# The factor of a gated recurrence's RMS norm as one power on GpSimd instead of a root on ScalarE and a reciprocal with correction on VectorE

## The chip, the cores and the metric

The kernel runs on one core of a Trainium2 chip. The metric is the device time of one execution in microseconds (us), the median of several runs. A core has four computing engines that work side by side and wait for one another through semaphores: TensorE (PE in the profile, with its weight loads as PEld), VectorE (DVE), ScalarE (ACT) and GpSimd (POOL). SyncE (SP) issues DMAs here. Each engine takes its instructions in a fixed order.

## The reference

Two layers, each a half-step SwiGLU feed-forward block, a mixing block with two branches, and a second feed-forward block, over 272 tokens (16 meta tokens and 256 of the sequence) of width 1024. One branch of the mixing block is multi-head attention with 8 heads over latent vectors, the other a gated linear recurrence with 4 heads of 128 channels. The change is in the norm at the recurrence's end:

```
o = o * lax.rsqrt(jnp.mean(o * o, axis=-1, keepdims=True) + EPS) * norm_w.astype(f32)
gate = jax.nn.silu(g_in.astype(f32)).reshape(B, L, HG_HEADS, HG_VDIM)
return (o * gate).reshape(B, L, HG_WIDTH).astype(dt)
```

For each head and token, the mean over 128 channels of the squares goes through a power of -1/2, and the result scales the head's output.

## The kernel before

Everything lies transposed: channels on the 128 partitions, tokens along the free dimension, 272 columns wide (256 in the last layer for all that only the 256 output tokens need). Each weight piece arrives by DMA in fp32 (`raw`) and is split into a rounded high part by ScalarE (`wh`, L191) and a low part by VectorE (`wl`, L192); activations are split in the same way (L217, L218). A product is then three fp32r matmuls (L212 to L214), and a tile of the projections into 128 channels is 24 of these in a row.

The code is written as Python generators that are advanced in turns, and each `yield` ends a turn. In the mixing block `weave("awr", ...)` takes one turn each of the attention (a: one head's scores, and the transposes of the head before), of the gate projections (w: one tile of 24 matmuls, with its evacuation by VectorE at L734) and of the recurrence (r). This sequence of turns is the program's order; a scheduler in the framework then moves instructions within the reach of their dependences, by its own estimates of their durations, and so fixes the order of each engine. A round below is one turn of each.

In the attention turn the two score blocks of a head (L769) go to PSUM; VectorE adds the mask (L771) and takes the row maximum (L773); ScalarE takes the exponential with a sum (L774); VectorE takes the sum's reciprocal (L775) and scales a part (L776, L781), ScalarE scales the other (L779, a copy with a scale); TensorE transposes the result `pm` (L787 to L789), and ScalarE evacuates it (L791). Behind the last exponential, `gate_on` (L1047) puts 16 sigmoids over the finished gate tiles, with a load of ScalarE's table ahead.

The recurrence's end is `outputs()`. Its last steps, in the program's order:

- the squares of the four heads' outputs are summed over channels by four matmuls (L998) into one PSUM tile, 32 partitions for each head;
- L1000, VectorE: `m`, the mean plus epsilon, 128x272;
- a `yield`, then `rsqrt` (L350): root on ScalarE (L353, with a table load before it and another, L774, before the next exponential), reciprocal on VectorE (L354); a `yield`; then on VectorE one step of Newton's correction, L356, L357 and L358, which writes the factor `rg`;
- four matmuls with `rowsel` (L1006) spread each head's factor over 128 partitions, two into PSUM tiles `aux`, two into `mm`;
- VectorE multiplies these with the gated outputs and the norm's weight (L1008), and the results are split (L217, L218) for the projection that follows after the attention's end.

`rsqrt` is used by the other norms too (`Norm.rstd`, `latent_norm`), which the change leaves alone. GpSimd does little: the diagonal blocks of the recurrence (L946), copies of the rotary key (L640), and, at the end of the program, two powers of 128x1 (L462) with `ex`, a column of -0.5.

Of the kernel before, what the change touches and what calls it, by code (L numbers as in the profile page):

```python
# [10 lines left out]
F32 = mybir.dt.float32  # L11
# [3 lines left out]
ALU = mybir.AluOpType  # L15
# [3 lines left out]
P = 128  # L19
# [4 lines left out]
L = SEQ + NM  # L24
# [28 lines left out]
def trunk(ctx: ExitStack, tc: tile.TileContext, a: dict):  # L53
# [5 lines left out]
    def T(shape, dt=F32, tag=None, bufs=1):  # L59
        counter[0] += 1  # L60
        return sb.tile(shape, dt, name=f"{tag}_{counter[0]}", tag=tag, bufs=bufs)

    def PS(tag="mm"):
        counter[0] += 1
        return pp.tile([P, 512], F32, name=f"p{tag}_{counter[0]}", tag=tag, bufs=4)
# [23 lines left out]
    @contextmanager  # L89
    def hold():  # L90
        Engine.held = True
        yield
        Engine.held = False

    V, S, E, GP = Engine(nc.vector), Engine(nc.scalar), Engine(nc.tensor), nc.gpsimd
# [4 lines left out]
    def act(dt=F32):  # L100
        return T([P, L], dt, "act", 44)

    def tmp(shape=(P, L), tag="tmp", bufs=7, dt=F32):
        return T(list(shape), dt, tag, bufs)
# [98 lines left out]
    def piece():  # L203
        used[0] += 1
        while len(ready) < min(used[0] + ahead[0], len(plan)):
            ready.append(prepare(*plan[len(ready)]))
        r, ready[used[0] - 1] = ready[used[0] - 1], None
        return r
# [12 lines left out]
    ones = T([P, P], F32, "ones")  # L221
    V.memset(ones, 1.0)
    busy = T([P, 1], F32, "busy")
    S.activation(out=busy, in_=ones[:, 0:1], func=AF.Sqrt)
    ps = PS("aux")
    for _ in range(11):
# [39 lines left out]
    def col(i):  # L266
        return cols[:, i:i + 1]
# [83 lines left out]
    def rsqrt(out, m, c):  # L351
        y, z = tmp(), tmp()
        S.activation(out=y[:, c], in_=m, func=AF.Sqrt)  # L353
        V.reciprocal(out=y[:, c], in_=y[:, c])  # L354
        yield
        V.tensor_tensor(out=z[:, c], in0=y[:, c], in1=y[:, c], op=ALU.mult)  # L356
        V.scalar_tensor_tensor(out=z[:, c], in0=z[:, c], scalar=-0.5, in1=m, op0=ALU.mult, op1=ALU.mult)  # L357
        V.scalar_tensor_tensor(out=out, in0=z[:, c], scalar=1.5, in1=y[:, c], op0=ALU.add, op1=ALU.mult)  # L358
# [86 lines left out]
    def ffn_out(norm, c):  # L445
        gain = [T([P, 512], F32, "vt", 3) for _ in range(2)]
        for i in range(2):
            src = a["vecs"][FN + 4 * i:FN + 4 * i + 4].rearrange("k p -> (k p)")
            nc.scalar.dma_start(out=gain[i], in_=src.unsqueeze(0).broadcast_to([P, 512]))

        fm = T([P, 2, 4], F32, "fm")
        ex = T([P, 1], F32, "ex")
        GP.memset(ex, -0.5)
        acts = ffn_up(norm, c)

        def square(t, ps):
            S.activation(out=sqs[:, t], in_=ps, func=AF.Square, accum_out=fm[:, t, 1:2])


        def store(t, n):  # L460
            r = fm[:, t, 3:4]
            GP.tensor_tensor(out=r, in0=r, in1=ex, op=ALU.pow)  # L462
            o, (g0, g1) = ot[:, t], scaled[t]
            S.activation(out=o[:, 0:n], in_=g0[:, 0:n], func=AF.Copy, scale=r)
            if n < 512:
                V.tensor_scalar(out=o[:, n:512], in0=g0[:, n:512], scalar1=r, scalar2=None, op0=ALU.mult)
            V.tensor_scalar(out=o[:, 512:D], in0=g1, scalar1=r, scalar2=None, op0=ALU.mult)
            for q, cc in ((nc.scalar, slice(0, n)), (nc.sync, slice(n, D))):
                q.dma_start(out=a["out"][0, t * P:(t + 1) * P, cc], in_=o[:, cc])

        scaled = [[], []]
        for hf in range(2):
            pst = [PS(), PS()]

            def prods(t, k0, w):
                ts_ = slice(t * P, (t + 1) * P)
                for k in range(k0, k0 + 2):
                    (ah, al), (wh, wl) = acts[k], w[k - k0]
                    E.matmul(pst[t], ah[:, ts_], wh, start=k == 0, stop=False)  # L479
                    E.matmul(pst[t], al[:, ts_], wh, start=False, stop=False)  # L480
                    E.matmul(pst[t], ah[:, ts_], wl, start=False, stop=k == NF - 1)  # L481

            held = []
            for k0 in range(0, NF, 2):
                w = piece()
                prods(0, k0, w)
                if hf and k0 >= NF - 6:
                    held.append((k0, w))
                else:
                    prods(1, k0, w)  # L490
                for t in range(2):
                    for k in range(4 if k0 == 0 else 0):
                        E.matmul(pst[t][:, k * P:(k + 1) * P], h[4 * hf + k][:, slice(*TOK[1 + t])], ident,
                                 start=False, stop=False)
            for k0, w in held:
                prods(1, k0, w)
            sqs, os = (T([P, 2, 512], F32, n) for n in ("gq", "gk" if hf else "gf"))
            if hf == 0:
                for t in range(2):
                    square(t, pst[t])  # L500
                    V.tensor_scalar(out=fm[:, t, 0:1], in0=fm[:, t, 1:2], scalar1=1.0 / D, scalar2=EPS,
                                    op0=ALU.mult, op1=ALU.add)
                    V.tensor_tensor(out=os[:, t], in0=pst[t], in1=gain[0], op=ALU.mult)
                    scaled[t].append(os[:, t])
        ot = T([P, 2048], F32, "raw", 3).rearrange("p (t d) -> p t d", t=2)
        for t in range(2):
            scaled[t].append(os[:, t])
        with hold():
            for t in range(2):
                square(t, pst[t])  # L510
                V.tensor_tensor(out=os[:, t], in0=pst[t], in1=gain[1], op=ALU.mult)
                V.scalar_tensor_tensor(out=fm[:, t, 3:4], in0=fm[:, t, 1:2], scalar=1.0 / D, in1=fm[:, t, 0:1],
                                       op0=ALU.mult, op1=ALU.add)
                store(t, 384 if t else 512)


    def mix(l, norm, nxt):
        last = l == DEPTH - 1
        ca = slice(0, L)
        cq = slice(NM, L) if last else ca  # L520
# [454 lines left out]
        def outputs():  # L975
            og, sqs = [], []
            pss = [PS(t) for t in ("aux", "aux", "mm", "mm")]

            for g in range(G):
                ms = slice(32 * g, 32 * g + NM)  # L980
                if not last:
                    E.matmul(pss[g][:, 0:NM], gv[0][ms], amm[ms], start=True, stop=True)
                E.matmul(pss[g][:, NM:L], gv[0][ms], am[ms], start=True, stop=False)
            for g in range(G):
                gs = slice(g * P, (g + 1) * P)
                ps = pss[g]
                E.matmul(ps[:, NM:L], gv[1][:, gs], at[:, g, 1:3], start=False, stop=False)
                E.matmul(ps[:, 144:L], gv[2][:, gs], at[:, g, 0], start=False, stop=True)
                sq, o = tmp(), act()
                S.activation(out=sq[:, cq], in_=ps[:, cq], func=AF.Square)  # L990
                V.tensor_tensor(out=o[:, cq], in0=ps[:, cq], in1=gate[g][:, cq], op=ALU.mult)
                og.append(o)
                sqs.append(sq)
                if g % 2:
                    yield
            ss = PS("aux")
            for g in range(G):
                E.matmul(ss[32 * g:32 * g + 32, cq], ones[:, 0:32], sqs[g][:, cq], start=True, stop=True)  # L998
            m, rg = tmp(), act()
            V.tensor_scalar(out=m[:, cq], in0=ss[:, cq], scalar1=1.0 / P, scalar2=EPS, op0=ALU.mult, op1=ALU.add)  # L1000
            yield
            yield from rsqrt(rg[:, cq], m[:, cq], cq)
            pss = [PS(t) for t in ("aux", "aux", "mm", "mm")]
            for g in range(G):
                gs = slice(32 * g, 32 * g + 32)
                E.matmul(pss[g][:, cq], rowsel[gs], rg[gs, cq], start=True, stop=True)  # L1006
            for g in range(G):
                V.scalar_tensor_tensor(out=og[g][:, cq], in0=pss[g][:, cq], scalar=col(HGN + l), in1=og[g][:, cq],  # L1008
                                       op0=ALU.mult, op1=ALU.mult)
                oh, ol = act(F32R), act(F32R)  # L1010
                split(og[g][:, cq], oh, ol, cq)
                ob.append((oh[:, cq], ol[:, cq]))
            yield
# [186 lines left out]
```

## Time and profile before

| what | value |
|---|---|
| median of 3 runs | 1212.39 us (1212.19 to 1212.58) |
| the profiled execution's own time | 1212.17 us |
| its span in the profile | 1210.1 us |
| PE busy, DVE busy | 1196.1 us (99%), 871.0 us (72%) |
| ACT busy, POOL busy | 647.6 us (54%), 27.9 us (2%) |
| `rsqrt` of the recurrence | once a layer, around 337 to 346 us and 938 to 947 us of the span |

Busy time is the time in which an engine executes instructions. A row of the timeline gives an instruction's start, its duration, its engine and line, what it writes and reads, and in brackets the idle time of the engine just before it with what ended that. Rows of one engine overlap a little, because the next instruction starts while the last is still writing. The matmuls of L769, L998, L1006 and L812, whose operands are plain fp32, stand in the trace as two rows each.

### The profile page before, as it was taken

To read this page: it belongs to the slowest core of one execution; us is meant where nothing else is said; L and a number is where in the kernel's file an instruction comes from. 1 tells how busy PE (TensorE), PEld (TensorE's weight loads), DVE (VectorE), ACT (ScalarE), POOL (GpSimd) and SP (SyncE) were. 2 spreads that over 40 slices of the span, in tenths; PEclk is the share of its full clock that TensorE was granted. 3 is DMA by queue.
4 is the path that set the end of the run, shared out by engine and by line. 5 is a ranking of instruction groups with operands and counts; after the bars stand their busy time and mean duration, and the time that the engine had idled before them with its cause. 6 is when DMAs were issued, how large, how long until landed. Compare 5 with 4: busy or idle time off the path is not lost.

```text
span 1210.1 us, 24079 instructions
## 1 busy us (share of the span) xinstructions
PE 1196.1 (99%) x10080; PEld 1164.9 (96%) x10080; DVE 871.0 (72%) x1533; ACT 647.6 (54%) x1068; POOL 27.9 (2%) x41
## 2 busy tenths in 40 slices
PE   9999999999999999999999999999999999999997
PEld 9999999999989999999999999999989899999986
DVE  7977655898787777775568776558877787877643
ACT  5644444676684554444445444446767745554432
POOL 2000000003000000000000000000020000000000
PEclk9999999999999999999999999999999999999999
DMA  8554655554435545555554646555554355555651
GB/s 264 175 194 155 200 187 159 156 162 143 138 113 167 174 141 185 163 193 179 187 174 140 200 149 200 185 159 164 156 173 135 126 172 183 172 179 172 209 190 53
DMA packets 187052, 203.49 MB, mean 168 GB/s; under 512 B 3412, under 2 KB 174624, under 8 KB 186944
## 3 DMA queue, kind: packets, MB, share of 16 engines
q1 hardware_dynamic: 186224, 200.87, 51.8%
q8 instruction: 79, 1.29, 0.5%
q10 hardware_dynamic: 720, 1.09, 0.3%
q14 instruction: 29, 0.24, 0.1%
HBM read 200.89 MB, written 1.05 MB: 167 GB/s over the span
## 4 chain that ended last, share of the span: by engine, by line
PE 96%; DVE 2%; ACT 1%; issue 0%; POOL 0%; POOLq 0%; DVEq 0%
PE pmm L212 21%; PE pmm L214 21%; PE pmm L213 20%; PE paux L212 7%; PE paux L213 7%; PE paux L214 6%; PE pmm L481 2%; PE pmm L479 2%; PE pmm L480 2%; PE paux L84 1%; PE paux L769 1%; PE pmm L84 1%; PE paux L404 0%; PE paux L407 0%; PE pmm L404 0%
## 5 line engine op out<-in xcount | busy, mean ns | idle before, releaser
L191 ACT CAST wh<-raw 128x1024 fp32r<-128x1024 f32 (+3 forms) x390 | 391.6, 1008 | 373.0 <-PE pmm L213 252.2
L192 DVE TENSOR_TENSOR wl<-raw,wh 128x1024 fp32r<-128x1024 f32 (+3 forms) x390 | 458.5, 1179 | 184.4 <-ACT wh L191 182.8
L212 PE MATMUL pmm<-x,wh 128*128 128x272 f32 (+1 forms) x1232 | 357.7, 290 | 0.0
L214 PE MATMUL pmm<-x,wl 128*128 128x272 f32 (+1 forms) x1232 | 352.1, 286 | 0.0
L213 PE MATMUL pmm<-x,wh 128*128 128x272 f32 (+1 forms) x1232 | 352.0, 286 | 0.0
L214 PE MATMUL pmm<-act,wl 128*128 128x272 f32 (+1 forms) x836 | 239.1, 287 | 1.6 <-DVE wl L192 1.5
L212 PE MATMUL pmm<-act,wh 128*128 128x272 f32 (+1 forms) x836 | 239.8, 287 | 0.0
L213 PE MATMUL pmm<-act,wh 128*128 128x272 f32 (+1 forms) x836 | 239.2, 286 | 0.0
L212 PEld LDWEIGHTS pmm<-x,wh 128*128 128x128 f32 x1232 | 232.2, 188 | 2.2 <-ACT wh L191 0.9
L213 PEld LDWEIGHTS pmm<-x,wh 128*128 128x128 f32 x1232 | 232.5, 189 | 0.5
L214 PEld LDWEIGHTS pmm<-x,wl 128*128 128x128 f32 x1232 | 232.1, 188 | 0.0
L213 PE MATMUL paux<-x,wh 128*128 128x272 f32 (+1 forms) x640 | 183.0, 286 | 0.0
L212 PE MATMUL paux<-x,wh 128*128 128x272 f32 (+1 forms) x640 | 182.9, 286 | 0.0
L214 PE MATMUL paux<-x,wl 128*128 128x272 f32 (+1 forms) x640 | 182.6, 285 | 0.0
L214 PEld LDWEIGHTS pmm<-act,wl 128*128 128x128 f32 x836 | 157.1, 188 | 1.7 <-DVE wl L192 1.6
L212 PEld LDWEIGHTS pmm<-act,wh 128*128 128x128 f32 x836 | 157.4, 188 | 0.3 <-issue 0.2
L213 PEld LDWEIGHTS pmm<-act,wh 128*128 128x128 f32 x836 | 157.4, 188 | 0.0
L214 PEld LDWEIGHTS paux<-x,wl 128*128 128x128 f32 x640 | 120.5, 188 | 0.0
L212 PEld LDWEIGHTS paux<-x,wh 128*128 128x128 f32 x640 | 120.3, 188 | 0.0
L213 PEld LDWEIGHTS paux<-x,wh 128*128 128x128 f32 x640 | 120.3, 188 | 0.0
L217 ACT CAST act<-tmp 128x272 fp32r<-128x272 f32 (+1 forms) x88 | 36.6, 416 | 126.7 <-DVE tmp L386 126.6
L382 DVE TENSOR_TENSOR tmp<-pmm,rstd 128x272 f32<-128x272 f32 (+1 forms) x88 | 38.3, 435 | 43.3 <-PE pmm L214 42.9
(303 smaller groups left out, 1218.2 us busy)
## 6 DMA issues: line engine op xcount, KB each, us to landing
raw<-ffn_w_gu SPq DMA_DIRECT2D x86, 1024.0 KB, 5.5
raw<-w_in SPq DMA_DIRECT2D x36, 1024.0 KB, 5.3
raw<-ffn_w_down SPq DMA_DIRECT2D x34, 1024.0 KB, 5.0
raw<-ffn_w_down SPq DMA_DIRECT2D x12, 768.0 KB, 4.3
raw<-w_out SPq DMA_DIRECT2D x8, 1024.0 KB, 4.9
raw<-w_proj_attn SPq DMA_DIRECT2D x4, 1024.0 KB, 5.1
raw<-w_proj_rec SPq DMA_DIRECT2D x4, 1024.0 KB, 5.2
raw<-w_ukv SPq DMA_DIRECT2D x2, 1024.0 KB, 5.0
```

What stands on the lines that cost most here:

```text
L84: self.last = f(*args, **kw)
L191: S.copy(out=hw, in_=x)
L192: V.tensor_tensor(out=lw, in0=x, in1=hw.bitcast(F32), op=ALU.subtract)
L212: E.matmul(ps, wh, xh, start=start, stop=False)
L213: E.matmul(ps, wh, xl, start=False, stop=False)
L214: E.matmul(ps, wl, xh, start=False, stop=stop)
L217: S.copy(out=hi_tile[:, c], in_=src)
L382: V.tensor_tensor(out=gt[:, c], in0=pg[:, c], in1=r[:, c], op=ALU.mult)
L479: E.matmul(pst[t], ah[:, ts_], wh, start=k == 0, stop=False)
L480: E.matmul(pst[t], al[:, ts_], wh, start=False, stop=False)
L481: E.matmul(pst[t], ah[:, ts_], wl, start=False, stop=k == NF - 1)
L769: E.matmul(ps[:, 0:n], qs[hd][0:DQK, TOK[i + 1][0]:TOK[i + 1][1]], kT[hd][0:DQK, 0:n], start=True, stop=True)
```

## The change

The recurrence's norm no longer calls `rsqrt`. One instruction on GpSimd raises `m` to the power of -0.5, elementwise over 128x272 (128x256 in the last layer), with the exponent broadcast from a column `mhalf`. Between `m` and the `rowsel` matmuls there were two `yield`s, and now there are three. `mhalf` is filled once at the start, and the tail's two powers of 128x1 read it in place of `ex`.

```
+    mhalf = T([P, 1], F32, "mhalf")
+    GP.memset(mhalf, -0.5)
...
-        ex = T([P, 1], F32, "ex")
-        GP.memset(ex, -0.5)
+        ex = mhalf
...
             V.tensor_scalar(out=m[:, cq], in0=ss[:, cq], scalar1=1.0 / P, scalar2=EPS, op0=ALU.mult, op1=ALU.add)
             yield
-            yield from rsqrt(rg[:, cq], m[:, cq], cq)
+            GP.tensor_tensor(out=rg[:, cq], in0=m[:, cq], in1=mhalf.broadcast_to([P, L])[:, cq], op=ALU.pow)
+            yield
+            yield
             pss = [PS(t) for t in ("aux", "aux", "mm", "mm")]
```

Lines behind the edits have moved by 2 or 3: L1006 is L1009 in the changed kernel, L774 is L775, L779 is L780, L1047 is L1050. The numbers in the names are buffers and differ between the kernels.

TensorE in the first layer, before: the end of a gate tile, the `rowsel` matmuls, then the scores of the eighth head and the transposes of the seventh (`pm_4439`, `pm_4440`).

```order
L213 MATMUL pmm_4463<-x_2550,wh_4342 128x272
L214 MATMUL pmm_4463<-x_2549,wl_4343 128x272
L1006 MATMUL paux_4499<-act_4378,cst_82 128x272
L1006 MATMUL paux_4500<-act_4378,cst_82 128x272
L1006 MATMUL pmm_4501<-act_4378,cst_82 128x272
L1006 MATMUL pmm_4502<-act_4378,cst_82 128x272
L769 MATMUL paux_4529<-act_3848,act_3587 128x144
L769 MATMUL paux_4537<-act_3848,act_3587 128x272
L787 MATMUL paux_4545<-ident_77,pm_4439 128x128
```

And after: the `rowsel` matmuls (L1009) stand behind the next gate tile, with the eighth head's transposes (`pm_4495`, `pm_4496`) right behind them.

```order
L213 MATMUL pmm_4519<-x_2552,wh_4407 128x272
L214 MATMUL pmm_4519<-x_2551,wl_4408 128x272
L1009 MATMUL paux_4550<-act_4380,cst_84 128x272
L1009 MATMUL paux_4551<-act_4380,cst_84 128x272
L1009 MATMUL pmm_4552<-act_4380,cst_84 128x272
L1009 MATMUL pmm_4553<-act_4380,cst_84 128x272
L788 MATMUL paux_4578<-ident_79,pm_4495 128x128
L789 MATMUL paux_4578<-ident_79,pm_4496 128x128
L790 MATMUL paux_4578<-ident_79,pm_4496 128x128
```

So one more round (the eighth head's two scores, three transposes and 24 matmuls of a gate tile) lies ahead of `rowsel`. In the last layer the same has moved in the same way.

ScalarE in the first layer, before, from the weight split that stands ahead of the root:

```order
L191 CAST wh_4466<-raw_4464 128x1024
L353 ACT_TABLE_LOAD
L353 ACTIVATE tmp_4435<-tmp_4377 128x272
L774 ACT_TABLE_LOAD
L774 ACTIVATE pm_4380,sm_4024<-paux_4382,sm_4024 128x144
L791 COPY ptt_4402<-paux_4398 128x384
L191 CAST wh_4552<-raw_4464 128x1024
L774 ACTIVATE pm_4381,sm_4024<-paux_4390,sm_4024 128x272
```

And after, from the same weight split: the root and the two table loads are gone, and the sixth head's two exponentials follow each other with their scaling.

```order
L191 CAST wh_4465<-raw_4463 128x1024
L792 COPY ptt_4404<-paux_4400 128x384
L775 ACTIVATE pm_4382,sm_4026<-paux_4384,sm_4026 128x144
L775 ACTIVATE pm_4383,sm_4026<-paux_4392,sm_4026 128x272
L780 ACTIVATE pm_4383<-pm_4383,sm_4026 128x256
L191 CAST wh_4520<-raw_4463 128x1024
```

ScalarE after, two rounds on, at the eighth head's exponentials:

```order
L775 ACTIVATE pm_4495,sm_4026<-paux_4497,sm_4026 128x144
L775 ACTIVATE pm_4496,sm_4026<-paux_4505,sm_4026 128x272
L1050 ACT_TABLE_LOAD
L1050 ACTIVATE act_3671<-act_3671 128x272
L780 ACTIVATE pm_4496<-pm_4496,sm_4026 128x256
L191 CAST wh_4623<-raw_4585 128x1024
```

The gates' table load and first sigmoid (L1050), which stood behind that head's scaling (L779), now stand between its last exponential and its scaling (L780). On GpSimd the power is one new row in each layer, behind the copies of the rotary key and ahead of nothing in the same layer.

## The prediction

> **What bounds the kernel now.** The page's first part comes first, then the busy time by stages around the two changed places, then the list of waits.
>
> ```profile
> PE 1196.1 (99%) x10080; PEld 1164.9 (96%) x10080; DVE 871.0 (72%) x1533; ACT 647.6 (54%) x1068; POOL 27.9 (2%) x41
> 326.00:377.00 51.00, 49.23 (x397) 45.56 (x396) 37.58 (x93) 34.02 (x74) 0.00 (x0) 1.00 0.32 104
> 927.00:975.00 48.00, 45.92 (x386) 42.40 (x385) 36.07 (x92) 33.78 (x74) 0.00 (x0) 1.00 0.37 122
> PE paux L1006 <- DVE act L358: 2.9, 2, 1.6
> PE paux L787 <- DVE pm L781: 0.9, 2, 0.5
> ```
>
> TensorE is busy for 99% of the span. So work taken from VectorE and ScalarE is worth nothing by itself; only TensorE's idle time can be won. In the stretches that hold the ends of the two recurrences (second and third row: length, then busy time of PE, PEld, DVE, ACT, POOL) TensorE idles 51.00 - 49.23 = 1.77 us and 48.00 - 45.92 = 2.08 us, **3.85 us** together. The waits explain it: 2.9 us at L1006 (the `rowsel` matmuls) for L358, the last step of `rsqrt`, and 0.9 us at L787 (a transpose) for the softmax scaling on VectorE. That is the ceiling of any gain here, 0.32% of the time.
>
> The timeline of the first layer shows where these waits come from, here TensorE's anchors.
>
> ```profile
> 335.59 0.67 PE L998 MATMUL paux<-tmp,ones 128*32 128x272 f32 x8
> 336.19 0.97 PE L769 MATMUL paux<-act,act 96*128 96x144 f32 x4
> 340.32 0.87 PE L769 MATMUL paux<-act,act 96*128 96x144 f32 x4
> 345.80 0.50 PE L1006 MATMUL paux<-act,cst 32*128 32x272 f32 x2 [1.28 <-DVE act L358]
> 351.51 0.30 PE L787 MATMUL paux<-ident,pm 128*128 128x128 f32 x1 [0.49 <-DVE pm L781]
> ```
>
> And the chain on VectorE and ScalarE in between:
>
> ```profile
> 336.38 0.44 DVE L1000 TENSOR_SCALAR tmp<-paux 128x272 f32<-128x272 f32 x1 [0.23 <-PE paux L998]
> 336.64 1.28 ACT L353 ACT_TABLE_LOAD   x1
> 337.94 0.43 ACT L353 ACTIVATE tmp<-tmp 128x272 f32<-128x272 f32 x1
> 338.38 1.28 ACT L774 ACT_TABLE_LOAD   x1
> 338.49 1.84 DVE L354 RECIPROCAL tmp<-tmp 128x272 f32<-128x272 f32 x1
> 342.61 0.42 DVE L356 TENSOR_TENSOR tmp<-tmp 128x272 f32<-128x272 f32 x1
> 343.28 0.43 DVE L357 SCALAR_TENSOR_TENSOR tmp<-tmp,tmp 128x272 f32<-128x272 f32 x1
> 345.32 0.43 DVE L358 SCALAR_TENSOR_TENSOR act<-tmp,tmp 128x272 f32<-128x272 f32 x1
> ```
>
> From `m` at 336.82 to the factor at 345.75 pass 8.93 us, of which `rsqrt`'s own five steps are only 0.43 + 1.84 + 0.42 + 0.43 + 0.43 = 3.55 us. The rest is queueing: the page's chain of waits runs through VectorE almost without a hole from L1000 to L787. VectorE is the bound for those 15 us, and TensorE pays for it at two places.
>
> **What the change removes.** Per layer, VectorE loses L354 and L356 to L358, 1.84 + 0.42 + 0.43 + 0.43 = 3.12 us, and ScalarE loses two table loads and the root, from 336.64 to 339.66, 3.0 us. The sixth head's exponentials, which stood behind these table loads, come up to 3 us earlier, its `pm` with them. Both engines then reach every later step of these rounds ahead of TensorE, so I take away both waits in each layer: 3.85 us.
>
> **What it moves.** `rowsel` goes one round back. The start of the sixth head's scores at 336.19 and of the seventh's at 340.32 give a round's length on TensorE, 4.13 us. Before, `rowsel` was due at 345.80 - 1.28 = 344.52, two rounds behind 336.19 (344.45). After, it is due at 336.19 + 3 x 4.13 = 348.58. The last layer has the same pattern:
>
> ```profile
> 937.26 0.97 PE L769 MATMUL paux<-act,act 96*128 96x144 f32 x4
> 941.24 0.87 PE L769 MATMUL paux<-act,act 96*128 96x144 f32 x4
> 937.45 0.42 DVE L1000 TENSOR_SCALAR tmp<-paux 128x256 f32<-128x256 f32 x1 [0.23 <-PE paux L998]
> ```
>
> A round is 3.98 us, so `rowsel` is due at 937.26 + 3 x 3.98 = 949.20. No DMA of SP moves in order. Behind `rowsel`, VectorE's four products (L1008) and the splits come some 2.5 us later by the clock than before. They are read only by the projection after the attention's end, but the attention's copy of the probabilities (L806) is queued behind them on VectorE:
>
> ```profile
> 355.50 0.44 DVE L806 COPY act<-paux 128x272 f32<-128x272 f32 x1
> 358.40 0.74 PE L812 MATMUL paux<-act,vt 32*128 32x272 f32 x8
> ```
>
> Its reader on TensorE starts nearly 3 us behind it; TensorE reaches that reader about 1.5 us sooner now. I count nothing for it; if that cover were gone, it would cost about a microsecond a layer.
>
> **A new wait.** The order after puts the eighth head's transposes right behind `rowsel`, and on ScalarE the gates' table load and first sigmoid now stand ahead of that head's scaling (L779). The fifth head's round tells how long a softmax takes from its scores; the gates' own rows give the rest.
>
> ```profile
> 331.45 0.87 PE L769 MATMUL paux<-act,act 96*128 96x144 f32 x4
> 334.61 0.20 ACT L774 ACTIVATION_READ_ACCUMULATOR pm<-paux,sm 128x1 f32 x1
> 335.10 0.51 ACT L779 ACTIVATE pm<-pm,sm 128x256 f32<-128x256 f32 x1 [0.29 <-DVE sm L775]
> 353.01 1.28 ACT L1047 ACT_TABLE_LOAD   x1
> 354.30 0.43 ACT L1047 ACTIVATE act<-act 128x272 f32<-128x272 f32 x1
> ```
>
> From the scores to the last exponential's end are 334.81 - 331.45 = 3.36 us; with the table load, the sigmoid and the scaling, 1.28 + 0.43 + 0.51, `pm` is ready 5.58 us behind the scores. TensorE needs it a round and the `rowsel` matmuls later, 4.13 + 0.7 + 0.11 = 4.94 us. By this the wait is 0.64 us. That round had an L192 and two L991 on VectorE ahead of its maximum, which the eighth head's hasn't, so it may also be nothing. I take 0.35 us a layer, 0.7 us in all.
>
> **The power itself.** No row shows a power of 128x272. What GpSimd shows:
>
> ```profile
> 2.54 0.10 POOL L453 MEMSET ex<- 128x1 f32 x1
> 9.71 1.10 POOL L319 TENSOR_TENSOR tmp<-h 128x272 f32<-128x272 f32 x1 [7.07 <-ACT h L84]
> 10.78 0.64 POOL L319 TENSOR_TENSOR nacc<-h 128x272 f32<-128x272 f32 x1
> 1205.21 0.56 POOL L462 TENSOR_TENSOR fm<-fm,ex 128x1 f32<-128x1 f32 x1 [3.57 <-DVE fm L84]
> ```
>
> The lower end is a multiplication of the same shape, 0.64 us, or 1.10 us beside a busy VectorE. The upper end takes all of the 128x1 power beyond a bare start (0.56 - 0.10 = 0.46 us) for one column, with no overlap of columns: 272 x 0.46 = 125 us. What counts is a limit between: GpSimd is idle here, the power can start when `m` is written, and TensorE asks for it at 348.58 - 336.82 = 11.76 us (first layer) and 949.20 - 937.87 = 11.33 us (last) later. Less 0.2 us for the two handovers (my estimate from L1000's 0.23 us of idling for L998), the power is covered up to **11.5 and 11.1 us**, about 41 ns a column. That is 10 to 17 times the multiplication and a tenth of the upper end. The nearest row in operation says that most of 0.56 us can be start and latency, the nearest row in shape says about 1 us. I take it as covered, some microseconds, and keep both ends: at T us beyond the cover, the time is 1212.17 - 3.85 + 2T - 22.6 = 1185.7 + 2T.
>
> There is a rule that speaks against it. The Trainium skill's GPSIMD Engine Reference, section "Performance pitfalls for Q7 kernels", gives a chain of dependent fp32 operations as 4 cycles an element on the chain, and its section "Specifications" 1.2 GHz. An estimate from that page: 272 x 4 / 1.2 = 0.91 us for each dependent step, so that 12 steps would fill the cover, and 40 steps, 36 us, would give about 1258 us by the formula. Whether the power's loop overlaps its columns, no run here shows; by the row of 0.56 us alone both remain possible.
>
> GpSimd's work also touches VectorE's. Beside the copies of L640 a weight split took longer than in the rounds of the change:
>
> ```profile
> 296.42 6.67 POOL L640 COPY act<-act 32x272 f32<-32x272 f32 x8
> 299.35 1.42 DVE L192 TENSOR_TENSOR wl<-raw,wh 128x1024 fp32r<-128x1024 f32 x1
> 336.94 1.22 DVE L192 TENSOR_TENSOR wl<-raw,wh 128x1024 fp32r<-128x1024 f32 x1
> ```
>
> That is 0.2 us a split, 0.6 us for the three that may fall beside the power, out of the 3.12 us that VectorE has won. I count it at nothing. The fill of `mhalf`, 0.10 us, goes ahead of the identity on GpSimd, whose first reader starts 2.8 us after it is ready, and the tail's powers keep their work:
>
> ```profile
> 2.29 0.29 POOL masks.py:199 TENSOR_SCALAR_AFFINE_SELECT ident<-ident 128x128 f32<-128x128 f32 x1
> 5.37 0.23 PE L81 MATMUL paux<-ident,rows 76*128 76x76 f32 x1
> ```
>
>
> **The sum.** 3.85 - 0.7 = 3.15 us less than the profiled execution's 1212.17, 1209.0 us; that execution is 0.22 us below the median of the runs, and I leave the result at **1209.0**.
>
> **The rivals.**
>
> - The power is covered, but the gain is smaller. The eighth head's transposes wait for ScalarE by the full 0.64 us or more, or VectorE is held up by GpSimd. For it speaks the table load ahead of L779, against it that the same softmax has fewer rows ahead of it. Losing 1 us more gives about 1210.2, less than 0.2% (2.4 us, about what a measurement of this kernel can tell from no change) below before.
> - The power is a little too long, 11.5 to 14.5 us. Then `rowsel` waits for GpSimd instead of VectorE: at 13.3 us the gain is gone (1212.3), at 14.5 us it is 1214.7.
> - Slower: the columns don't overlap, or only partly. Place: `rowsel` in each layer, TensorE idle, everything behind it late. It decides from T = 14.5 us and costs 2 us for each microsecond beyond. T = 20 gives 1225.7, a quarter of the full 0.46 us a column (31 us) 1248, the full value 1436. For it speaks that the one column took 0.46 us over a bare start, as much as 190 columns of the 0.64 us multiplication; against it that this row can't tell start from work.
> - The change does nothing that counts, because the scheduler moved `rowsel` anyway and another wait of VectorE follows: 1212. The two waits listed are the only ones here, so I give it little, within the first rival.
>
> **How the numbers follow.** Covered with the full gain: 0.56, own range 1207.9 to 1209.7 (no new wait, 1208.3 less 0.4 for the scatter; up to 0.2% of gain). Covered with a smaller gain: 0.10. T between 11.5 and 14.5 us: 0.10. Longer: 0.24, of which 0.17 lies above 20 us. The range runs from 1207.9 to 1226, which leaves out these 0.17 and a little below. Faster by more than 0.2%: 0.56 and a little of the third case, 0.57. Within 0.2%: 0.10 and most of 0.10, 0.18. Slower: 0.25.
>
> **What would show it.** GpSimd's row at the changed line gives T at once; under 11 us it is covered. TensorE's wait list should have lost L1006 for L358 in both layers and hold nothing for GpSimd; a wait of the last head's second and third transposes for ScalarE of 0 to 0.7 us would be the new one. The stretches 326 to 375 and 927 to 973 should show less than 0.7 us of TensorE idle in each. VectorE's busy time should fall by 6.2 us, ScalarE's by 6.0. The prediction is wrong if T is above 12 us, or if VectorE slows beside the power by more than its 3.12 us.

## The result and the profile after

The changed kernel takes 1276.48 us (median of 4 runs, 1275.64 to 1277.47) against 1212.49 us before: ratio **1.0528**, 95% interval 1.0514 to 1.0542. It is 64 us slower, far outside the range of the prediction.

The busy times of the changed kernel's page, its two longest waits of TensorE from the list of waits (engine and line, what it waited for, us in total, times, longest), and GpSimd's two powers from the timeline:

```profile
PE 1198.6 (94%) x10080; PEld 1167.7 (92%) x10080; DVE 867.3 (68%) x1525; ACT 642.9 (50%) x1062; POOL 114.7 (9%) x43
PE paux L1009 <- POOL act L1003: 64.4, 2, 33.3
PE pmm L214 <- DVE wl L192: 1.5, 1, 1.5
336.86 44.76 POOL L1003 TENSOR_TENSOR act<-tmp,mhalf 128x272 f32<-128x272 f32 x1 [33.91 <-DVE tmp L1001]
970.93 42.18 POOL L1003 TENSOR_TENSOR act<-tmp,mhalf 128x256 f32<-128x256 f32 x1 [33.52 <-DVE tmp L1001]
```

The powers take **44.76 and 42.18 us**. TensorE's busy time is what it was, its share of the span fell from 99 to 94%, and one wait explains it: `rowsel` (now L1009) waits 64.4 us for GpSimd. The waits for L358 and L781 are gone. TensorE's first `rowsel` row and the stretches around it, with the granted clock in the third column from the right (1.00 is full):

```profile
381.67 0.82 PE L1009 MATMUL paux<-act,cst 32*128 32x272 f32 x2 [33.25 <-POOL act L1003]
348.75:351.75 3.00, 0.00 (x0) 0.00 (x0) 0.15 (x1) 1.11 (x2) 3.00 (x1) 1.00 0.00 0
351.75:354.00 2.25, 0.00 (x0) 0.00 (x0) 0.00 (x0) 0.00 (x0) 2.25 (x1) 0.59 0.00 0
354.00:381.00 27.00, 0.00 (x0) 0.00 (x0) 0.00 (x0) 0.00 (x0) 27.00 (x1) 0.50 0.00 0
381.00:385.00 4.00, 3.33 (x18) 2.63 (x19) 2.02 (x6) 1.49 (x5) 0.62 (x1) 0.50 0.00 0
386.00:387.00 1.00, 1.00 (x9) 1.00 (x8) 0.93 (x3) 1.00 (x4) 0.00 (x0) 0.86 0.00 0
387.00:389.00 2.00, 2.00 (x17) 1.83 (x16) 1.25 (x4) 1.64 (x4) 0.00 (x0) 1.00 0.51 110
```

TensorE asks for the factor at 381.67 - 33.25 = 348.42 us and stands still for 33 us; from 351.75 us on nothing but GpSimd is busy. The granted clock drops to a half on the way: the mean of 0.59 over 351.75 to 354.00 puts the drop at 352.15 us, 3.7 us into the idling, and the mean of 0.86 over 386 to 387 puts the return at 386.28 us, 4.6 us after work resumes. In the last layer (asked for at 982.03 us, resumed at 1013.16), by the same working, the two delays are 5.0 and 4.6 us. So a long wait is paid for twice: once for itself, once in the work right behind it.

### The profile page after: what moved, and what is told of

The parts are those of the page before. It is cut to its first block, busy times and chain, and to the rows that moved or that the text cites. A ratio compares the mean times of both kernels' runs of the same rounds, so it can differ in the third digit from the quotient of the medians.

```text
span 1273.8 us, 24072 instructions
## 1 busy us (share of the span) xinstructions
PE 1198.6 (94%) x10080; PEld 1167.7 (92%) x10080; DVE 867.3 (68%) x1525; ACT 642.9 (50%) x1062; POOL 114.7 (9%) x43
## 3 DMA queue, kind: packets, MB, share of 16 engines
HBM read 200.89 MB, written 1.05 MB: 159 GB/s over the span
## 4 chain that ended last, share of the span: by engine, by line
PE 91%; POOL 7%; ACT 1%; issue 0%; DVE 0%; POOLq 0%; DVEq 0%
PE pmm L212 20%; PE pmm L213 19%; PE pmm L214 19%; POOL act L1003 7%; PE paux L212 6%; PE paux L213 6%; PE paux L214 6%; PE pmm L481 1%; PE pmm L482 1%; PE pmm L480 1%; PE paux L84 1%; PE paux L770 1%; PE pmm L84 1%; PE paux L406 0%; PE pmm L409 0%; PE paux L409 0%
## 5 line engine op out<-in xcount | busy, mean ns | idle before, releaser
L192 DVE TENSOR_TENSOR wl<-raw,wh 128x1024 fp32r<-128x1024 f32 (+3 forms) x390 | 458.5, 1179 | 183.6 <-ACT wh L191 182.2
L1003 POOL TENSOR_TENSOR act<-tmp,mhalf 128x272 f32<-128x272 f32 (+1 forms) x2 | 86.9, 43468 | 67.4 <-DVE tmp L1001 67.4
```

What stands on the lines that cost most here:

```text
L192: V.tensor_tensor(out=lw, in0=x, in1=hw.bitcast(F32), op=ALU.subtract)
L1003: GP.tensor_tensor(out=rg[:, cq], in0=m[:, cq], in1=mhalf.broadcast_to([P, L])[:, cq], op=ALU.pow)
```

## The experiments

Theory A: the change loses by the length of the power alone, what of it is left when TensorE asks for the factor; all else that it does is good. The rivals are named with each run. The runs came in three batches, each beside its own runs of the kernel before (medians 1212.6 to 1213.1 us). The kernels in which a multiplication stands in for the power, on the whole tile or on a part of it, and the one with another exponent compute a different factor; they serve for the time alone.

**The later place of `rowsel`, without the power.** The kernel before, with one line more:

```
             yield from rsqrt(rg[:, cq], m[:, cq], cq)
+            yield
             pss = [PS(t) for t in ("aux", "aux", "mm", "mm")]
```

> The kernel before with one more yield behind its rsqrt, so that the rowsel matmuls stand a round later, as in the changed kernel; root, reciprocal and correction stay on ScalarE and VectorE. Theory A (the change loses only by the length of the power, and its place in the order is good): the waits of 1.28 and 1.64 us at rowsel go, those of 0.9 us for the softmax may stay, so 1208.5 to 1209.8 us. Rival B (the later place itself costs, by the transposes right behind rowsel and by later products on VectorE): 1212 us or more.

Measured: **1208.43 us**, ratio 0.9968 (0.9956 to 0.9981). Its stretches (length, then busy time of PE, PEld, DVE, ACT, POOL) and its one wait that is left there:

```profile
326.00:377.00 51.00, 50.71 (x410) 47.44 (x410) 38.49 (x95) 35.20 (x75) 0.00 (x0) 1.00 0.32 111
927.00:975.00 48.00, 47.70 (x405) 44.46 (x404) 36.84 (x90) 33.91 (x73) 0.00 (x0) 1.00 0.39 132
PE paux L787 <- DVE pmc L776: 0.6, 2, 0.3
```

TensorE idles 0.29 and 0.30 us where it idled 1.77 and 2.08. With every instruction of `rsqrt` still in place, the place alone recovers 3.3 of the 3.85 us. This kernel is faster than the kernel before and than the changed one, so rival B (the later place costs) falls.

**The change with a short instruction on GpSimd.** The power's operation is replaced by a multiplication:

```
-... in1=mhalf.broadcast_to([P, L])[:, cq], op=ALU.pow)
+... in1=mhalf.broadcast_to([P, L])[:, cq], op=ALU.mult)
```

> The changed kernel with a multiplication by the exponent in place of the power, so the factor is not a power of the mean; all else as changed. Theory A: GpSimd's row falls from 44.8 to about 1 us, TensorE's idle time in the two stretches falls under 0.7 us each, 1208.3 to 1209.2 us: the time that the prediction gave for a covered power. Rival B (something else of the change costs): 1212 us or more.

Measured: 1208.04 us, ratio 0.9962 (0.9948 to 0.9975).

```profile
337.89 1.67 POOL L1003 TENSOR_TENSOR act<-tmp,mhalf 128x272 f32<-128x272 f32 x1 [33.91 <-DVE tmp L1001]
326.00:377.00 51.00, 51.00 (x413) 47.66 (x412) 37.05 (x91) 32.85 (x72) 1.67 (x1) 1.00 0.31 109
927.00:975.00 48.00, 48.00 (x411) 45.16 (x410) 35.81 (x89) 31.32 (x70) 1.66 (x1) 1.00 0.40 135
```

TensorE has no idle time left in either stretch. Had the power been covered, the change would have won the whole ceiling; rival B (something else in it costs) falls. Beside `e1_round`, all the work that the change takes off VectorE and ScalarE is worth 0.4 us by the medians and 0.6 us by the idle time that is gone.

**The same at the old place.** As before, with one of the two yields behind the multiplication taken out:

> As e2_mult (a multiplication in place of the power), with one yield fewer, so that rowsel stands where it stood before the change. If taking the work off VectorE and ScalarE is enough by itself, the factor is there 3 us behind the mean and 4 us ahead of rowsel, and the time is 1208 to 1209 us, as with the later place. If the gain needs the later place (because VectorE still holds up the softmax there), 1210.5 us or more.

Measured: 1210.23 us, ratio 0.998 (0.9971 to 0.9989), so half the gain. The timeline shows one wait of TensorE that has grown, and the chain on VectorE that it waits for (rows in between left out):

```profile
351.19 0.30 PE L788 MATMUL paux<-ident,pm 128*128 128x128 f32 x1 [0.92 <-DVE pm L782]
345.69 0.91 DVE L1010 SCALAR_TENSOR_TENSOR act<-paux,cols,act 128x272 f32<-128x272 f32 x2 [0.21 <-PE pmm L1008]
...
348.80 0.43 DVE L218 TENSOR_TENSOR act<-act,act 128x272 fp32r<-128x272 f32 x1
...
349.50 1.21 DVE L192 TENSOR_TENSOR wl<-raw,wh 128x1024 fp32r<-128x1024 f32 x1
350.63 0.23 DVE L777 TENSOR_SCALAR pmc<-pm,sm 128x16 f32<-128x16 f32 x1
350.76 0.28 DVE L782 TENSOR_SCALAR pm<-pm,sm 128x128 f32<-128x128 f32 x1
```

Here `rowsel` doesn't wait at all, but the four products and four splits that follow it (L1010, L218) stand on VectorE amid the eighth head's softmax, with a weight split (L192) as the last of the queue, and make it late. With the later place they come behind it: in `e2_mult` the first product starts at 350.14 us, the softmax's last step on VectorE at 348.60. Removing the first wait lets the second grow from 0.5 to 0.9 us a layer; only the place removes both.

**How long a power is, and where it stops being covered.** The power on the first n columns, a multiplication on the others, for n = 56 and 112:

```
+            c1, c2 = slice(cq.start, cq.start + 56), slice(cq.start + 56, L)
+            GP.tensor_tensor(out=rg[:, c2], in0=m[:, c2], in1=mhalf.broadcast_to([P, L])[:, c2], op=ALU.mult)
+            GP.tensor_tensor(out=rg[:, c1], in0=m[:, c1], in1=mhalf.broadcast_to([P, L])[:, c1], op=ALU.pow)
-            GP.tensor_tensor(out=rg[:, cq], in0=m[:, cq], in1=mhalf.broadcast_to([P, L])[:, cq], op=ALU.pow)
```

> The changed kernel with the power on the first 56 columns only, the other columns are multiplied by the exponent instead. Theory A (0.16 us a column from 44.76 us at 272 and 42.18 us at 256 columns, 0.4 us of start): the power's row takes 9.4 us, with the product 9.9 us, inside the cover of 11 us, so as e2_mult within 0.5 us, 1208.3 to 1209.5 us. Rival C (most of the 44 us is a start that does not depend on the width): 1270 us or more.

> The same with the power on 112 columns. Theory A: the power's row takes 18.4 us, with the product 18.9 us; rowsel waits 18.9 less the cover of 11.5 and 11.1 us, 7.4 and 7.8 us, so 1208.3 + 15.2 = 1223.5 us, plus 0 to 3 us if TensorE runs at a lower clock behind the wait, as it does in the changed kernel. Rival C: 1270 us or more.

Measured: 1208.28 us (ratio 0.9964, 0.9952 to 0.9977) and 1229.33 us (1.014, 1.0126 to 1.0154). The product and the power of 56 columns in the first layer, the power of 112 columns, and the second kernel's wait:

```profile
337.97 1.57 POOL L1004 TENSOR_TENSOR act<-tmp,mhalf 128x216 f32<-128x216 f32 x1 [33.91 <-DVE tmp L1001]
339.51 9.34 POOL L1005 TENSOR_TENSOR act<-tmp,mhalf 128x56 f32<-128x56 f32 x1
339.32 18.23 POOL L1005 TENSOR_TENSOR act<-tmp,mhalf 128x112 f32<-128x112 f32 x1
PE paux L1011 <- POOL act L1005: 16.8, 2, 8.6
```

From 56 to 112 columns the row grows by 8.89 us, 0.159 us a column; from 112 to 272 by 26.53 us, 0.166 us a column. The length is in the width and not in a start (rival C falls). A row of 9.34 us behind a product of 1.57 us costs nothing, one of 18.23 us makes TensorE wait 8.2 and 8.6 us in the two layers, 16.8 us in all: the cover lies where the prediction put it. The time with 112 columns was expected lower, 1223.5 to 1226.5 us: the waits are 1.6 us longer than the expected 15.2. From 1208.04 us they give 1224.8, and the 4.5 us that remain are more than the 0 to 3 us allowed for the clock. They are the next question.

**The lower clock behind the wait.** In the changed kernel, 1208.04 + 64.4 = 1272.4 us leave 4.0 us of the median open. TensorE is kept busy through the wait by matmuls that nobody reads, first 33, then 37:

```
             yield
             yield
+            fill = PS("aux")
+            for _ in range(33):
+                E.matmul(fill, ones, cst[:, 0:512], start=True, stop=True)
```

> The changed kernel with 33 matmuls of 128x512 whose result nobody reads, ahead of the rowsel matmuls, so that TensorE is busy while it waits for the power. They should take 28 to 33 us a layer, about as long as the wait (33.3 and 31.1 us). Theory A (the wait of 64.4 us accounts for 1208.3 + 64.4 = 1272.7 us, and the 2.9 us beyond that in the profiled execution of the changed kernel are TensorE's lower clock behind the wait): the granted clock stays at 1.00 and the time is 1272 to 1274 us, faster than the changed kernel although more is computed. Rival D (the 2.9 us are the products and splits queued up behind rowsel): 1275.5 us or more.

> As e4_fill with 37 filling matmuls in place of 33. In e4_fill they took 28.5 us a layer, so 4.9 us (first layer) of idling were left and the granted clock still fell to 0.50. 37 take 32.0 us: TensorE idles about 1.4 us in the first layer and not at all in the last, where the filling is some 0.8 us too long. Theory A (the clock behind the wait costs the 2.9 us): the clock stays near 1.00 and the time is 1208.3 + 33.4 + 32 = 1273.7 us, 1273 to 1274.5. Rival D (queued work): 1275.2 us or more.

Measured with 33: 1275.2 us (ratio 1.0515, 1.0499 to 1.053), which doesn't decide, since waits of 4.9 and 2.8 us were left and the clock dropped in both layers all the same, here in the first:

```profile
PE paux L1012 <- POOL act L1003: 7.7, 2, 4.9
378.00:382.00 4.00, 0.01 (x2) 0.01 (x2) 0.00 (x0) 0.00 (x0) 3.94 (x1) 0.76 0.00 0
382.00:386.00 4.00, 4.00 (x21) 3.29 (x22) 2.70 (x8) 1.95 (x5) 0.00 (x0) 0.50 0.00 0
```

Measured with 37: **1273.21 us** (1.05, 1.0486 to 1.0515), 3.3 us less than the changed kernel, with 74 matmuls more. Its stretches where work resumes:

```profile
377.00:382.00 5.00, 3.74 (x9) 1.33 (x7) 0.00 (x0) 0.00 (x0) 5.00 (x1) 1.00 0.00 0
382.00:386.00 4.00, 3.77 (x33) 3.41 (x34) 3.01 (x8) 1.95 (x5) 0.18 (x1) 1.00 0.00 0
PE paux L1012 <- POOL act L1003: 1.5, 1, 1.5
```

The clock stays at 1.00, and from 382 to 386 us 33 rows of matmuls start, where the changed kernel starts 22 at 0.50, though its work resumed earlier (at 381.67 us, here at 382.23):

```profile
382.00:386.00 4.00, 4.00 (x22) 3.30 (x19) 3.02 (x7) 2.49 (x8) 0.00 (x0) 0.50 0.00 0
```

In the last layer the filling ends 0.6 us behind the power, so about 3.3 + 0.6 = 3.9 of the 4.0 us are accounted for. So the remainder is the clock, and rival D (queued work) falls. The kernel with 112 columns fits: full clock returns there 4.1 and 6.3 us after work resumes, which at half speed costs some 5 us by estimate, and 4.5 were open. The Trainium skill's page "TensorE: Matmul & The Clock Gate", section "Part 1: The HAM clock gate (the "warmup" mystery)", gives a gate at half rate after an idle window of about 3.4 us, and full rate after a busy one. The traces agree with windows of that length: the stretches at 0.50 last 34.1 and 30.7 us in the changed kernel, 10.2 us in both layers with 112 columns and 6.8 us in `e5_late`, which is 10, 9, 3 and 2 times 3.41 us. They don't show a fixed delay: in these three kernels the drop comes 2.0 to 5.0 us into the idling and the return 4.1 to 6.3 us after work resumes. A wait of 2.8 us was enough for a drop (last layer with 33 matmuls, where the drop came after work had resumed), one of 1.5 us was not.

**`rowsel` as late as it can be.** Sixteen yields in place of the two put it behind the projection of the attention's branch, right ahead of the recurrence's own:

> The changed kernel with 16 yields behind the power in place of two, so that the rowsel matmuls stand behind the whole projection of the attention's branch, right ahead of the recurrence's own projection. Theory A (a power costs only what is left of its length when TensorE asks for it): rowsel is due some 41.4 us behind the mean in the first layer and 39.2 in the last, so TensorE waits about 3.4 and 3 us, and then some 2 us more for the products and splits that the projection reads; 1208.3 + 10.4 = 1218.7 us, 1216 to 1223 us with the clock. Rival E (GpSimd's long instruction slows VectorE beside it, over a shared path to the memory): 1230 us or more, with longer rows on VectorE between 337 and 381 us.

Measured: 1224.31 us (ratio 1.0095, 1.0078 to 1.0112), with these waits of TensorE, and VectorE's weight splits beside the power (minimum, median, maximum in ns), there and in the kernel before:

```profile
PE paux L1009 <- POOL act L1003: 8.6, 2, 4.5
PE pmm L212 <- ACT act L217: 2.0, 2, 1.0
382.00:386.00 4.00, 2.50 (x13) 1.73 (x14) 2.22 (x6) 1.34 (x4) 0.42 (x1) 0.50 0.00 0
386.00:390.00 4.00, 4.00 (x24) 4.00 (x23) 2.04 (x4) 0.31 (x1) 0.00 (x0) 0.67 0.36 124
L192 DVE TENSOR_TENSOR wl<-raw,wh x11: 1214/1224/1226, 337.6 to 376.0; 128x1024 fp32r<-128x1024 f32 x11
L192 DVE TENSOR_TENSOR wl<-raw,wh x11: 1205/1225/1227, 336.9 to 378.2; 128x1024 fp32r<-128x1024 f32 x11
```

The same power costs 16 us in place of 68, because 40 us of other work lie beside it in the first layer (from its start at 337.66 us to 377.95, when TensorE asks). The expectation (1216 to 1223 us) was a little low: the waits of 10.6 us give 1218.6, and some 6 us at half clock behind each wait (0.50 up to 386, 0.67 in the mean from there to 390) give the rest. Rival E falls: the eleven weight splits beside the power take as long as without it.

**What the power's length hangs on.** Three looks: the exponent as a whole tile in place of the broadcast column (`in1=mf[:, cq]`, filled ahead of time), the exponent 1.0 (`ones[:, 0:1]` in place of `mhalf`), and, behind a multiplication over the whole tile (L1003), two powers on different partitions, each on half of the columns:

```
+            c1, c2 = slice(cq.start, 144), slice(144, L)
+            for ps_, cc in ((slice(0, 64), c1), (slice(64, P), c2)):
+                GP.tensor_tensor(out=rg[ps_, cc], in0=m[ps_, cc], in1=mhalf.broadcast_to([P, L])[ps_, cc], op=ALU.pow)
```

> The changed kernel with the exponent in a whole tile of 128x272, filled by GpSimd, in place of the broadcast column. Theory A (the power is computed column by column, 0.16 us each, whatever its operands): GpSimd's row stays at 44.8 and 42.2 us and the time at 1276 us. Rival F (the broadcast operand makes the instruction slow): the row falls to a few us and the time to 1209 us.

> The changed kernel with 1.0 as exponent in place of -0.5, so the factor is the mean itself. If the power's loop does the same for every value, GpSimd's rows stay at 44.8 and 42.2 us; if its length hangs on the exponent, they get shorter and the time with them.

> The changed kernel with a multiplication over the whole tile and then two powers, one of partitions 0 to 63 on the first 144 (128) columns, one of partitions 64 to 127 on the other 128; the power is left out for the other two quarters. If the instructions run one after the other, 23.6 and 21 us, the rows add up to 44.6 us and the time stays at 1276 to 1279 us. If GpSimd's parts for different partitions work independently, the two overlap, rowsel waits until some 25.5 us behind the mean, 14 us in each layer, and the time is 1208.3 + 28 + 4 = 1240 us.

Measured: 1278.59 us, 1275.96 us (one run each) and 1278.93 us (ratio 1.0545, 1.0524 to 1.0566). GpSimd's rows in the first layer, in this order; for the third kernel both halves are in one row, and the grouped view gives the mean of one in ns:

```profile
338.01 44.92 POOL L1005 TENSOR_TENSOR act<-tmp,act 128x272 f32<-128x272 f32 x1 [33.50 <-DVE tmp L1001]
338.20 44.76 POOL L1003 TENSOR_TENSOR act<-tmp,ones 128x272 f32<-128x272 f32 x1 [33.90 <-DVE tmp L1001]
338.98 44.13 POOL L1006 TENSOR_TENSOR act<-tmp,mhalf 64x144 f32<-64x144 f32 x2
L1006 POOL TENSOR_TENSOR act<-tmp,mhalf 64x128 f32<-64x128 f32 x3 | 62.2, 20719 | 0.2
```

Neither the broadcast (rival F) nor the choice between -0.5 and 1.0 as exponent matters. The first kernel is 2 us slower than the changed one, of which its rows explain 0.3 us; it is a single run, and the rest stays open. Half the partitions don't make a column shorter (20.72 us for 128 columns are 0.16 us each), and the two halves run one after the other: their lengths, 23.3 and 20.7 us, fill the row of 44.13 us.

## Why the prediction was wrong

- **The step that failed is the power's length, T in the prediction's sum.** The prediction had the ends 0.64 and 125 us and took "covered, some microseconds", so T of at most 11.5 and 11.1 us. Measured were 44.76 and 42.18 us, about four times that. It allowed that most of the 0.56 us of the 128x1 power could be start, and that was so: by estimate some 0.4 us are start (9.34 - 56 x 0.16) and 0.16 us are the one column. But to be covered, a column had to take 41 ns at most, and 0.16 us are four times as much. The upper end, 0.46 us a column, was 2.8 times too long. 0.16 us is a number that a 128x1 row can't give, since it can't tell start from work.
- **The slower rival had the mechanism, the place and the price.** `rowsel` waits in each layer for what the cover leaves. With the measured lengths, the formula gives 1185.7 + 44.76 + 42.18 = 1272.6 us, against 1275.64 us of the profiled execution; the missing 3 us are the clock behind the wait, which the formula hadn't. The rival's chance of 0.24 was too small for a row that allowed 31 or 125 us as well as 1 us.
- **The estimate from the Trainium skill's GPSIMD Engine Reference**, section "Performance pitfalls for Q7 kernels", pointed the right way: for 40 dependent steps, 36 us and 1258 us, it was the nearest of the times that the prediction named. That it came so near is luck, since nothing gave the 40. That the 0.16 us of a column are such a chain is not shown; no run here could separate a long chain from many operations.
- **The bound and the ceiling were right.** Without the power (`e2_mult`) the span falls by 1210.1 - 1206.2 = 3.9 us, the whole idle time of the two stretches; the forecast had been 3.85.
- **The place of `rowsel` was right.** It was to be due at 348.58 us and was asked for at 348.42, and the cover of 11 us was confirmed from both sides by 56 and 112 columns. The price of 2 us for each microsecond beyond the cover holds as far as the waits go (8.2 and 8.6 us with 112 columns).
- **What the gain comes from was half wrong.** The prediction credited it to the work taken off VectorE and ScalarE. `e9_near`, with that work gone and the old place, wins only half; `e1_round`, with the work in place and the later place, nearly all.
- **The new wait of 0.35 us a layer isn't there.** No run with the later place shows TensorE waiting for L780. The exponentials came earlier than in the round that the estimate was taken from: in `e2_mult` the last one ends 2.56 us behind the start of the scores (345.26 to 347.82 us), not 3.36, and the scaling ends at 349.95 us, just ahead of the transposes at 350.05.
- **The power did not slow VectorE's weight splits**, as assumed: 1224 ns a split with the power beside it, 1225 ns without.
- **VectorE's busy time fell by 3.7 us instead of 6.2, ScalarE's by 4.7 instead of 6.0.** The rows that went are as long as forecast: summed row by row, VectorE has 6.4 us less in `e2_mult` than before and ScalarE 6.0. Busy time counts rows that overlap only once, and they overlap less in the new order.

## What to carry to other kernels

An instruction that moves to an idle engine is free only as long as its length fits between the moment its input is there and the moment its reader asks; work that gap out, and if no row gives the length at the full width, treat a row of one element as a warning and not as a price. Before a wait is bought off with another engine, try a later place for its reader: here one `yield` was worth 4.2 us (1212.62 to 1208.43), with nothing else changed. And when TensorE would wait for some 3 us or more, count the first 4 to 6 us of work behind the wait at half the clock, 2 to 3 us for each wait here.

## What was not expected of the hardware

- GpSimd's power takes 0.16 us for each column, some 70 times a column of the multiplication of the same shape before (0.64 us for 272) and 27 times one of the multiplication in its own place (1.67 us), alike for the exponents -0.5 and 1.0, for 64 and 128 partitions, and for a broadcast and a whole exponent tile.
- Two powers on different halves of the partitions don't overlap: 23.3 and 20.7 us, end to end.
- A power of 45 us leaves the length of VectorE's two-input weight splits beside it as it was (1224 and 1225 ns), while a split of 1.42 us in place of 1.22 had stood beside shorter GpSimd copies.
